# Two-layer HGRN2 + RWKV-7 trunk: the places of the conditioning columns, of the decay path's casts and of silu(c)

## The chip, the cores and the metric

The kernel runs on one NeuronCore of one Trainium2 chip. The metric is device time in microseconds (us) of one execution; the kernel is run several times and the median counts. Everything is float32; matmul operands are split into a high and a low part (`hi`, `lo`, both in the format fp32r), so that three matmuls (hi·hi, hi·lo, lo·hi) make one accurate product.

## What is computed

Two layers over 512 tokens of width 1024. Each layer first needs a conditioning vector of 3 × 1024 numbers from `c`:

```python
cond = silu(c) @ w_ada[l] + b_ada[l]
shift, scale, gate_raw = split(cond, 3)
h = x * (1 + scale) + shift
p_hg, p_rw, p_gate = split(h @ w_in[l], [...])
y_hg = HGRN2(p_hg) * silu(z_hg) @ w_branch_hg[l]
y_rw = RWKV7(p_rw) * silu(z_rw) @ w_branch_rw[l]
merged = sigmoid(g_hg) * y_hg + sigmoid(g_rw) * y_rw
x = layer_norm(ALPHA * x + (1 + gate_raw) * (merged @ w_out[l]))
```

`shift` and `scale` of a layer must be there before its projection starts. `gate_raw` is needed only at that layer's end. So in layer 0 the kernel has time to make layer 0's eight gate columns and layer 1's sixteen shift and scale columns (a column is 128 of the 1024 numbers, one per partition) beside other work.

## The kernel before, in words

**A column** (`ada_col`, line 308) is made on VectorE (DVE). A 128 × 1024 block of `w_ada` is loaded in two halves by two DMAs (`ada_next`, line 327, on the queue of SP). Each half is multiplied with half of silu(c) and summed along the row by one fused instruction (in the trace `CUSTOM_DVE_ANT_0`, in the order of instructions `ISA`), each followed by a short read of the accumulator, and a last small addition joins the halves. silu(c), copied to all partitions, lies in two tiles, `silc`. `ada_next` first computes the columns that are pending, then starts the loads of the next ones, so a column is loaded one call ahead of its use. Tiles named `z` (four of them) hold the halves.

**A layer** goes through these stages:

1. The four pairs. For `p` = 0 to 3 one HGRN2 head (`hg_head`) and one preparation of two RWKV heads (`rw_prep`) are made. Both are long chains of small steps on DVE, ScalarE (ACT), GpSimd (POOL) and TensorE (PE). Between the steps, `weave` places `fill`: matmuls of the projection tiles that come next (lines 267, 268 and 272), in numbers that tables set for each step. PE runs its instructions in that fixed order, so a late DVE step makes PE wait, and the fill behind it too. In the first pair `rw_wa` makes the RWKV decay and rate from the 64-wide down projections `wad`: two tiles `x[i]` get a cast of one half of the partitions (line 381) and a subtraction for the other half, and eight pairs of matmuls (lines 393, 394) read them.
2. `rw_invert`: a triangular inversion, all on DVE, with fill on PE.
3. Eight chunks (`rw_chunk`) of the RWKV recurrence, with fill; each makes one column in layer 0, its two halves pinned at two places (`side`).
4. The branch stage, for `j` = 0 to 7: two projections `pa` and `pb` (weights `w_br`), then on DVE two `SCALAR_TENSOR_TENSOR` that read them out of PSUM (lines 1170 and 1171, shown as line 135), their sum (line 1172) and `hilo`: ACT casts the high part, DVE subtracts for the low part (line 126). `out1(j - 1)` then multiplies the previous tile with the first half of `w_out`. Weights come through three `raw` tiles on SP's queue, are cast by ACT (line 121, `wh<-raw`), and POOL makes the low part (line 126, `wl<-raw,wh`).
5. The layer's end, which is joined with the start of the next layer.

**What sets the order.** The program is written as one stream per engine and a scheduler orders it by priority. `tc.issue_after(x)` makes the instructions of the block stand behind `x` if they are on the same engine as `x`. It adds no wait, and it does not bind other engines: the loads of a column may go earlier.

**The columns before.** In the pairs of layer 0 `ada_next` is called after each `weave` (lines 1075 and 1087), eight times for one column each (`WAZ`), and nothing pins those instructions. The scheduler put all eight of them in the stretch from the middle of the first pair to the beginning of the second. Eight more are made in the chunks, and eight in the branch stage (`WAB`), there behind the sum of line 1172 (`merged`).

**silu(c).** Before the chunks, ACT copies `silc` to two other tiles, `keep`, since the chunks use its memory. After the chunks `keep` is given up, and at the start of the branch stage `c` is loaded again (line 1161), spread over all partitions, and `c_rows` computes silu again: a tanh on ACT and a `SCALAR_TENSOR_TENSOR` on DVE for each half.

Of the kernel before, what the change touches and what calls it, by code (L numbers as in the profile page):

```python
# [12 lines left out]
F32 = mybir.dt.float32  # L13
F32R = mybir.dt.float32r
U8 = mybir.dt.uint8
AF = mybir.ActivationFunctionType
ALU = mybir.AluOpType
AX = mybir.AxisListType

WAZ = (1, 1, 1, 1, 1, 1, 1, 1)  # L20
WAB = (1, 1, 1, 1, 1, 1, 1, 1, 0)
NWARM = 5
ORD = ((11, 2), (3, 20), (4,), (5, 6), (21,7), (8,), (), ())

# [58 lines left out]
def body(ctx, tc, d):  # L83
# [20 lines left out]
    def u(shape=(128, 512), dt=F32):  # L104
        return st("u", list(shape), dt)

    def big(tag, dt=F32R):
        return st(tag, [128, 4, 2, 512], dt)
# [16 lines left out]
    def tt(e, o, a, b, op):  # L125
        return e.tensor_tensor(o, a, b, op=op)  # L126

    def mul(e, o, a, b):
        return tt(e, o, a, b, ALU.mult)
# [7 lines left out]
    def bc(ap, n):  # L137
        return ap.unsqueeze(len(ap.shape)).broadcast_to(list(ap.shape) + [n])
# [237 lines left out]
    def rw_wa(l, wad):  # L376

        x = [st("z", [128, 512], F32R) for _ in range(2)]
        for i in range(2):
            r, q = slice(64 * i, 64 * i + 64), slice(64 - 64 * i, 128 - 64 * i)  # L380
            V.tensor_copy(x[i][r], wad[r])
            tt(V, x[i][q], wad[r], x[i][r].bitcast(F32), ALU.subtract)
        wu = [wunit(d["up"][l, i], *(("X", "X") if l else ("pu", "pu"))) for i in range(2)]
        for i in range(2):

            G.memset(wu[i][1][64 - 64 * i:128 - 64 * i].bitcast(F32), 0.0)
        rw["gt"], rw["vm"] = [], []
        for p in range(NP):
            cols = slice(p * 128, (p + 1) * 128)
            g = st("t4" if p < 3 else "G", [128, 2, 512])  # L390
            for i, bias in ((0, "w0"), (1, "a0")):
                pw = ps("rw")
                yield mm(pw, wu[i][0][:, cols], x[i], start=True, stop=False)
                yield mm(pw, wu[i][1][:, cols], x[i], start=False, stop=True)
                act(g[:, i], pw, AF.Tanh, scale=0.5, bias=P(bias, l, p))
            rw["gt"].append(g)
# [22 lines left out]
        shift(x, pst, l, c)  # L419
        return x  # L420

    def rw_prep(l, p, r, k, v, after):

        sg, th = rw["gt"][p][:, 0], rw["gt"][p][:, 1]
        if l == 1:
# [8 lines left out]
        ts(G, sg, sg, 0.5, 0.5, ALU.mult, ALU.add)  # L434
        cum = pu()
        with tc.issue_after(after[0].ins):
            V.tensor_tensor_scan(cum, mask64, sg, 0.0, ALU.mult, ALU.add)
        EP = ep
        EI = cum
        with tc.issue_after(after[1].ins):  # L440
# [64 lines left out]
                mm(pA[h][ro:ro + 64, c4i * 64:(c4i + 1) * 64], ZR[hs, zc:zc + 64], BK[hs, zc:zc + 64],  # L505
                   start=c4i == 0, stop=c4i == 3)
        for h in range(2):
            mul(V, ar[:, h, p], pA[h][:, 0:256].rearrange("p (c j) -> p c j", j=64), bc(d2[:, :, p, h], 64))

        pT = ps("rw")  # L510
        for t in range(4):
# [174 lines left out]

    def hilo(y, o, e=G):
        act(o[:, 0], y, AF.Copy)
        tt(e, o[:, 1], y, o[:, 0].bitcast(F32), ALU.subtract)

    def rw_gate(l, p, pz):
        z, t = st("z", [128, 512]), u()
# [308 lines left out]
    for l in range(L):  # L1001
# [62 lines left out]
        for p in range(NP):  # L1064
            early = []
            if p:
                fill = itertools.chain(fqi(p, hgp), krv(p, rkv))
            elif l:
                fill = itertools.chain(fqi(p, hgp), wa(), krv(p, rkv))
            else:  # L1070
                fill = itertools.chain(krv(p, rkv), rw_wa(l, wad), fqi(1, early, 1))
            weave(hg_head(l, p, hgp, oT, ends := []), fill, (WHL if l else WHZ, WHG if l else WHS, WHG, WHG)[p])
            run(fill)
            if l == 0:
                ada_next(*itertools.islice(ada, WAZ[2 * p]))
            if p == 0:
                rw["vtm"] = [st("X", [128, 512]) for _ in range(8)]
            hgp = early
            if p < 3:
                fill = fqi(p + 1, hgp, 3 if early else 2)  # L1080
            else:
                fill = itertools.chain.from_iterable(
                    [gate(j) for j in range(5)] + [zrw(p) for p in range(NP)] + [zhg(p) for p in range(NP)] +
                    [gate(j) for j in range(5, KT)])
            weave(rw_prep(l, p, rkv[1], rkv[0], rkv[2], ends), fill, WPR)
            if l == 0:
                ada_next(*itertools.islice(ada, WAZ[2 * p + 1]))
            if p < 3:
                run(fill)
            rkv = []  # L1090
        ada_next()

        piece[:] = [512]
        keep = [hl(), st("pr", [128, 512])]
# [8 lines left out]
        for c in range(8):  # L1103
            ada_next(*itertools.islice(ada, 1), tag="u")
            weave(rw_chunk(l, c, ada_parts()), fill, WCH, 1000)
        o_hg, y_rw = big(tag_r), big(tag_r)

        def finish():
            with tc.high_priority(offset=1000):
# [46 lines left out]

        xa, ow, wo = [], [], []
        if l == 0:
            craw = [u(), u()]
            for h in range(2):  # L1160
                nc.sync.dma_start(craw[h], d["c"][h * 512:(h + 1) * 512].partition_broadcast(128))
            c_rows(craw)
            ada_next(*itertools.islice(ada, WAB[0]))
        if l == 1:
            n0, nrm = norm_rows(0), norm_rows(1)
        for j in range(KT):
# [4 lines left out]
            stt(mc, gates[j][1], 1.0, pb, ALU.add, ALU.mult)  # L1171
            merged = V.tensor_tensor(ma, ma, mc, op=ALU.add)
            with tc.issue_after(merged.ins):
                hilo(ma, mg[j], V)
            ow.append(wunit(d["w_out"][l, j * 128:(j + 1) * 128, 0:512]))
            if j:
                wo.append(wo_unit(j - 1))
                out1(j - 1)
            with tc.issue_after(merged.ins):
                if l == 0:  # L1180
                    ada_next(*itertools.islice(ada, WAB[j + 1]))
                elif j % 2 == 0:
                    x1_rows(j // 2)
# [210 lines left out]
```

## Time and profile before

| | |
|---|---|
| median of 3 runs | 996.07 us (994.84 to 997.43) |
| the profiled execution | 997.83 us, of which the span from the first to the last instruction is 996.0 us |
| mean granted clock of TensorE over the span | 0.977 of full speed |
| PE busy | 943.5 us (95% of the span) |
| DVE busy | 733.2 us (74%) |
| ACT, POOL busy | 453.8 us (46%), 602.9 us (61%) |

The pairs of layer 0 lie at about 57 to 230 us, its inversion to 283, its chunks to 390, its branch stage at 411 to 478; layer 1 starts at about 520. A row of a timeline gives start, duration, engine, line, operation, tiles and count, and in brackets how long the engine stood idle before it and which instruction ended that idle time. An idle time of PE costs time; an idle time of another engine costs time only where PE comes to wait for that engine. A matmul of 128 × 512 lasts 0.39 us in these rows at full clock, but the next starts before it ends.

### The profile page before, as it was taken

The numbers are of one execution on the slowest core, as the hardware profiler recorded it, in microseconds if no ns is written. First come the engines' busy times: TensorE is split into PE (matmuls) and PEld (weight loads), VectorE is DVE, ScalarE is ACT, GpSimd is POOL, SyncE is SP. The second block draws the span as 40 slices with busy tenths as digits, with TensorE's granted clock in tenths as the row PEclk, the third lists the DMA queues.
The fourth block names the chain that finished last, engine by engine and source line by source line (L and its number), as shares of the span: only waits on it lengthen the run. The fifth ranks groups of instructions, "written<-read, shape, count | busy, mean of one in ns | idle before, by whom it ended". The sixth has DMA issues, their size and how long they took to land.

```text
span 996.0 us, 16762 instructions
## 1 busy us (share of the span) xinstructions
PE 943.5 (95%) x6132; PEld 762.2 (77%) x6132; DVE 733.2 (74%) x1265; ACT 453.8 (46%) x924; POOL 602.9 (61%) x580
## 2 busy tenths in 40 slices
PE   7979899999998999999989999999999899999996
PEld 4757788887876777778878777888787677777775
DVE  7888986769974766487876686767899376746767
ACT  3356465465334335433444655555632443353421
POOL 5466657556445666666545577666642566675665
PEclk9998999999998999999999999999999899999998
DMA  9824332322322341656632122222231333355322
GB/s 315 315 64 148 116 86 75 92 74 85 99 76 84 98 117 44 173 187 190 193 119 64 54 85 85 75 82 77 75 96 64 96 107 97 108 171 166 114 78 84
DMA packets 61748, 112.83 MB, mean 113 GB/s; under 512 B 6865, under 2 KB 11361, under 8 KB 61666
## 3 DMA queue, kind: packets, MB, share of 16 engines
q1 hardware_dynamic: 57778, 105.12, 34.0%
q10 hardware_dynamic: 3888, 6.64, 2.0%
q8 instruction: 48, 0.79, 0.3%
q14 instruction: 34, 0.28, 0.1%
HBM read 106.49 MB, written 5.25 MB: 112 GB/s over the span
## 4 chain that ended last, share of the span: by engine, by line
PE 63%; DVE 25%; DMA 4%; ACT 3%; issue 3%; POOL 2%; SPq 0%; DVEq 0%; POOLq 0%; ACTq 0%
PE ppj L272 14%; PE ppj L267 13%; PE ppj L268 13%; DVE t L126 5%; DVE t L541 3%; DVE B L308 2%; DVE t L533 2%; PE prw L597 2%; DVE u L126 1%; POOL wl L126 1%; PE prw L616 1%; PE ppj L1194 1%; PE ppj L1196 1%; PE ppj L1195 1%; PE prw L621 1%
## 5 line engine op out<-in xcount | busy, mean ns | idle before, releaser
L126 POOL TENSOR_TENSOR wl<-raw,wh 128x256 fp32r<-128x256 f32 (+1 forms) x321 | 348.1, 1099 | 268.0 <-ACT wh L121 135.3
L121 ACT ACTIVATE wh<-raw 128x512 fp32r<-128x512 f32 (+1 forms) x233 | 144.1, 622 | 166.6 <-PE ppj L268 103.0
L267 PE MATMUL ppj<-B,wh 128*128 128x512 f32 x432 | 174.7, 404 | 1.8 <-DVE u L135 1.8
L268 PE MATMUL ppj<-B,wh 128*128 128x512 f32 x432 | 172.2, 399 | 0.0
L267 PE MATMUL ppj<-A,wh 128*128 128x512 f32 x400 | 163.1, 408 | 0.0
L268 PE MATMUL ppj<-A,wh 128*128 128x512 f32 x400 | 161.4, 403 | 0.0
L272 PE MATMUL ppj<-B,wl 128*128 128x512 f32 x432 | 125.5, 401 | 0.0
L272 PE MATMUL ppj<-A,wl 128*128 128x512 f32 x400 | 118.3, 407 | 2.4 <-POOL wl L126 2.4
L267 PEld LDWEIGHTS ppj<-B,wh 128*128 128x128 f32 x432 | 82.0, 190 | 18.9 <-ACT wh L121 2.6
L272 PEld LDWEIGHTS ppj<-B,wl 128*128 128x128 f32 x432 | 81.0, 190 | 17.1
L268 PEld LDWEIGHTS ppj<-B,wh 128*128 128x128 f32 x432 | 82.1, 190 | 14.9
L272 PEld LDWEIGHTS ppj<-A,wl 128*128 128x128 f32 x400 | 75.3, 193 | 20.2 <-POOL wl L126 4.5
L267 PEld LDWEIGHTS ppj<-A,wh 128*128 128x128 f32 x400 | 76.7, 192 | 16.0 <-ACT wh L121 0.3
L268 PEld LDWEIGHTS ppj<-A,wh 128*128 128x128 f32 x400 | 76.9, 192 | 14.1
L126 DVE TENSOR_TENSOR t<-t,t 128x144 f32<-128x144 f32 (+29 forms) x62 | 44.3, 715 | 2.1
L126 POOL TENSOR_TENSOR hl<-hl,u 128x256 f32<-128x256 f32 x40 | 32.0, 800 | 20.0 <-DVE u L787 9.2
L135 DVE SCALAR_TENSOR_TENSOR pr<-ppj,prm,pr 128x511 f32<-128x511 f32 x22 | 16.5, 748 | 30.2 <-ACT pr L123 30.2
L126 DVE TENSOR_TENSOR W<-prw,d 64x256 f32<-64x256 f32 x32 | 13.5, 422 | 33.7 <-PE prw L621 33.2
L126 DVE TENSOR_TENSOR hl<-hl,u 128x256 f32<-128x256 f32 x64 | 31.9, 519 | 2.6 <-ACT u L805 1.3
L516 ACT COPY X<-prw 64x128 f32<-64x128 f32 x64 | 16.7, 261 | 25.4 <-PE prw L512 24.7
L541 DVE TENSOR_REDUCE t<-t 128x4 f32<-128x4 f32 (+30 forms) x62 | 26.4, 425 | 2.1
L126 DVE TENSOR_TENSOR u<-u 128x256 f32<-128x256 f32 (+6 forms) x56 | 25.5, 456 | 0.7
(484 smaller groups left out, 2009.8 us busy)
## 6 DMA issues: line engine op xcount, KB each, us to landing
raw<-in_w_in SPq DMA_DIRECT2D x182, 256.0 KB, 2.6
B<-in_w_ada SPq DMA_DIRECT2D x16, 512.0 KB, 6.2
z<-in_w_ada SPq DMA_DIRECT2D x32, 256.0 KB, 3.4
u<-in_w_ada SPq DMA_DIRECT2D x32, 256.0 KB, 3.5
raw<-in_w_br SPq DMA_DIRECT2D x32, 256.0 KB, 2.7
raw<-in_w_out SPq DMA_DIRECT2D x32, 256.0 KB, 2.7
u<-in_x SPq DMA_DIRECT2D x8, 256.0 KB, 4.4
o<-in_w_in SPq DMA_DIRECT2D x14, 128.0 KB, 4.7
```

Source lines behind the costliest of these rows:

```text
L121: A.activation(out, in_, f, scale=scale)
L126: return e.tensor_tensor(o, a, b, op=op)
L135: V.scalar_tensor_tensor(o, a, s, b, op0=op0, op1=op1)
L267: yield mm(o, w, xh, start=half == 0 and k == 0, stop=False)
L268: yield mm(o, w, xl, start=False, stop=False)
L272: yield mm(o, w, xh, start=False, stop=half == n - 1 and k == 3)
L308: V.tensor_tensor_reduce(out=w[h], in0=w[h], in1=silc[h], scale=0.5, scalar=0.0 if h else init, op0=ALU.mult, op1=ALU.add, accum_out=part[ ...
L516: A.copy(rw["vtm"][2 * t + e][r:r + 64, p * 128:(p + 1) * 128], pT[64 * e:64 * e + 64, t * 128:(t + 1) * 128])
L533: V.transpose(Tin[qs].rearrange("p t s -> p s t"), ax[qs, :, cs_].rearrange("p h s -> p s h"))
L541: V.tensor_reduce(blk(R, t, [32, j]), pv, axis=AX.X, op=ALU.add)
L597: mm(pg[h][:, p * 128:(p + 1) * 128], BK[p][hs, ch], ZR[p][hs, ch], start=p == 0, stop=p == 3)
L616: mm(py[:, p * 128:(p + 1) * 128], ZR[p][:, ch], mbd[:, p], start=p == 0, stop=False)
```

## The change

There are four edits.

- **The columns in the pairs of layer 0.** `ada_next` is now called inside `rw_prep` at two places: `side(0)`, pinned behind the scan on DVE, and `side(1)`, pinned behind the last multiplication of the preparation (`ar`). `WAZ` starts five columns instead of eight, none at the first place of the first pair, and as a column is computed one call after its load, the first pair computes none. The other three are made later: the chunks still take eight, and `WAB` gives the branch stage eleven instead of eight, two at every second tile.
- **The branch stage's pins.** Columns (in layer 1, the rows of `x1`) stand behind the low part's subtraction (`low`) and no more behind `merged`.
- **The casts of the decay path** (line 381) go from DVE to ACT, in both layers.
- **silu(c)** is copied back from `keep` by ACT after the chunks, instead of being loaded and computed again.

```diff
-WAZ = (1, 1, 1, 1, 1, 1, 1, 1)
-WAB = (1, 1, 1, 1, 1, 1, 1, 1, 0)
+WAZ = (0, 1, 1, 1, 1, 1, 0, 0)
+WAB = (1, 2, 1, 2, 1, 2, 1, 1, 0)
...
             r, q = slice(64 * i, 64 * i + 64), slice(64 - 64 * i, 128 - 64 * i)
-            V.tensor_copy(x[i][r], wad[r])
+            act(x[i][r], wad[r], AF.Copy)
             tt(V, x[i][q], wad[r], x[i][r].bitcast(F32), ALU.subtract)
...
-    def rw_prep(l, p, r, k, v, after):
+    def rw_prep(l, p, r, k, v, after, side):
...
-            V.tensor_tensor_scan(cum, mask64, sg, 0.0, ALU.mult, ALU.add)
+            scan = V.tensor_tensor_scan(cum, mask64, sg, 0.0, ALU.mult, ALU.add)
+        with tc.issue_after(scan.ins):
+            side(0)
...
-            mul(V, ar[:, h, p], pA[h][:, 0:256].rearrange("p (c j) -> p c j", j=64), bc(d2[:, :, p, h], 64))
+            last = mul(V, ar[:, h, p], pA[h][:, 0:256].rearrange("p (c j) -> p c j", j=64), bc(d2[:, :, p, h], 64))
+        with tc.issue_after(last.ins):
+            side(1)
...
-        tt(e, o[:, 1], y, o[:, 0].bitcast(F32), ALU.subtract)
+        return tt(e, o[:, 1], y, o[:, 0].bitcast(F32), ALU.subtract)
...
-            if l == 0:
-                ada_next(*itertools.islice(ada, WAZ[2 * p]))
...
-            weave(rw_prep(l, p, rkv[1], rkv[0], rkv[2], ends), fill, WPR)
-            if l == 0:
-                ada_next(*itertools.islice(ada, WAZ[2 * p + 1]))
+            side = lambda i: ada_next(*itertools.islice(ada, 0 if l else WAZ[2 * p + i]))
+            weave(rw_prep(l, p, rkv[1], rkv[0], rkv[2], ends, side), fill, WPR)
...
-        ada_next()
...
         o_hg, y_rw = big(tag_r), big(tag_r)
+        if l == 0:
+            silc[:] = [mbd.rearrange("p a b -> p (a b)"), st("W", [128, 512])]
+            for h in range(2):
+                A.copy(silc[h], keep[h])
...
         if l == 0:
-            craw = [u(), u()]
-            for h in range(2):
-                nc.sync.dma_start(craw[h], d["c"][h * 512:(h + 1) * 512].partition_broadcast(128))
-            c_rows(craw)
             ada_next(*itertools.islice(ada, WAB[0]))
...
             with tc.issue_after(merged.ins):
-                hilo(ma, mg[j], V)
+                low = hilo(ma, mg[j], V)
...
-            with tc.issue_after(merged.ins):
+            with tc.issue_after(low.ins):
                 if l == 0:
                     ada_next(*itertools.islice(ada, WAB[j + 1]))
```

**DVE in the first pair of layer 0**, where the HGRN2 head begins (`hl`, `phg` and `prw` are its tiles, `z` the decay path's). Before:

```order
L126 TENSOR_TENSOR u_630<-u_605 128x256
L381 CAST z_706<-u_613 64x512
L126 TENSOR_TENSOR hl_628<-phg_669,cc 128x512
L787 COPY u_677<-hl_606 128x64x2
L126 TENSOR_TENSOR hl_627<-hl_627,u_630 128x128x2
```

and now:

```order
L126 TENSOR_TENSOR u_630<-u_605 128x256
L126 TENSOR_TENSOR z_706<-u_613,z_706 64x512
L126 TENSOR_TENSOR hl_628<-phg_669,cc 128x512
L792 COPY u_677<-hl_606 128x64x2
L126 TENSOR_TENSOR hl_627<-hl_627,u_630 128x128x2
```

The cast has left DVE, and the decay path's subtraction stands in its place. PE's two `L792` matmuls of that level, which need the copy, now stand behind three matmuls of line 272 instead of one.

**SP's queue in the branch stage of layer 0**, where the tiles' weights (`raw`) and the columns (`z`) are loaded. Before:

```order
L1150 DMA raw_4426<-in_w_out 128x512
L327 DMA z_4448<-in_w_ada 128x512
L327 DMA z_4449<-in_w_ada 128x512
L252 DMA raw_4453<-in_w_br 128x512
L252 DMA raw_4472<-in_w_br 128x512
L252 DMA raw_4497<-in_w_out 128x512
```

and now:

```order
L1155 DMA raw_4404<-in_w_out 128x512
L327 DMA z_4349<-in_w_ada 128x512
L327 DMA z_4350<-in_w_ada 128x512
L327 DMA z_4426<-in_w_ada 128x512
L327 DMA z_4427<-in_w_ada 128x512
L252 DMA raw_4435<-in_w_br 128x512
L252 DMA raw_4454<-in_w_br 128x512
L252 DMA raw_4479<-in_w_out 128x512
```

Four halves of columns now stand ahead of the next tile's two `w_br` loads where two stood. This comes three times in the stage; between them it is two as before.

**DVE at the start of layer 1's branch stage** (`B` is the tile of `hilo`, `bv` and `o` are the rows of `x1`, `raw` is the second half of `w_out`, which this layer multiplies with the gate row `X`). Before:

```order
L1172 TENSOR_TENSOR u_9168<-u_9168,u_9169 128x512
L126 TENSOR_TENSOR bv_9181<-bv_9181,z_9114 128x512
L126 TENSOR_TENSOR o_9185<-o_9185,z_9115 128x512
L126 TENSOR_TENSOR bv_9181<-bv_9181,z_9116 128x512
L126 TENSOR_TENSOR o_9185<-o_9185,z_9117 128x512
L126 TENSOR_TENSOR B_9112<-u_9168,B_9112 128x512
L135 SCALAR_TENSOR_TENSOR u_9227<-hl_7352,ppj_9189 128x512
L126 TENSOR_TENSOR raw_9240<-raw_9240,X_9105 128x512
```

and now:

```order
L1173 TENSOR_TENSOR u_9162<-u_9162,u_9163 128x512
L126 TENSOR_TENSOR raw_9234<-raw_9234,X_9099 128x512
L135 SCALAR_TENSOR_TENSOR u_9221<-hl_7346,ppj_9183 128x512
L126 TENSOR_TENSOR B_9106<-u_9162,B_9106 128x512
L126 TENSOR_TENSOR bv_9175<-bv_9175,z_9108 128x512
L126 TENSOR_TENSOR o_9179<-o_9179,z_9109 128x512
```

The rows of `x1` now follow the low part, as the new pin asks, but the multiplication of `raw` has come ahead of it.

## Rows read from the trace of the kernel before

**Rows 1.** The page's chain that ended last: shares of the span by engine

```profile
PE 63%; DVE 25%; DMA 4%; ACT 3%; issue 3%; POOL 2%; SPq 0%; DVEq 0%; POOLq 0%; ACTq 0%
```

**Rows 2.** Windows, first pairs of both layers: busy us (instructions), PEclk, DMA share, GB/s

```profile
60.00:120.00 60.00, 50.03 (x259) 39.83 (x258) 54.80 (x110) 32.42 (x76) 39.40 (x47) 0.92 0.44 136
530.00:590.00 60.00, 56.21 (x317) 45.71 (x317) 46.79 (x77) 35.60 (x79) 39.05 (x46) 1.00 0.23 67
```

**Rows 3.** Timeline of DVE in the first pair of layer 0

```profile
70.05 2.60 DVE L381 CAST z<-u 64x512 fp32r<-64x512 f32 x1
72.57 0.67 DVE L126 TENSOR_TENSOR hl<-phg,cc 128x512 f32<-128x512 f32 x1
73.17 0.21 DVE L787 COPY u<-hl 128x128 f32<-128x128 f32 x1
...
75.76 0.69 DVE L126 TENSOR_TENSOR z<-u,z 64x512 fp32r<-64x512 f32 x1
```

**Rows 4.** Timeline of POOL at the same place

```profile
70.27 2.09 POOL L126 TENSOR_TENSOR wl<-raw,wh 128x256 fp32r<-128x256 f32 x3
```

**Rows 5.** Waits of PE, 55 to 130 us: us in total, times, longest

```profile
PE prw L792 <- DVE u L787: 3.2, 1, 3.2
PE phg L763 <- DVE u L126: 2.6, 3, 1.6
PE prw L505 <- DVE B L135: 1.6, 1, 1.6
PE prw L816 <- ACT u L808: 1.0, 1, 1.0
```

**Rows 6.** Timeline of PE: matmuls before and after a wait

```profile
113.23 0.39 PE L267 MATMUL ppj<-A,wh 128*128 128x512 f32 x1
113.46 0.39 PE L268 MATMUL ppj<-A,wh 128*128 128x512 f32 x1
...
117.44 0.63 PE L267 MATMUL ppj<-A,wh 128*128 128x512 f32 x1
117.87 0.63 PE L268 MATMUL ppj<-A,wh 128*128 128x512 f32 x1
```

**Rows 7.** Windows of line 308 alone on DVE, 60 to 122 us: sum

```profile
sum 62.00, DVE 13.66; mean DVE 4.55
```

**Rows 8.** Timeline of DVE in the third pair and at the fourth's start

```profile
171.69 0.69 DVE L126 TENSOR_TENSOR pu<-pr,pu 128x512 f32<-128x512 f32 x1 [1.32 <-POOL pu L132]
...
193.10 0.50 DVE L126 TENSOR_TENSOR u<-u,u 128x256 f32<-128x256 f32 x1 [2.71 <-ACT u L730]
```

**Rows 9.** Timelines of DVE and PE, start of layer 0's branch stage

```profile
417.85 0.69 DVE L135 SCALAR_TENSOR_TENSOR mbd<-mbd,u 128x512 f32<-128x512 f32 x1 [2.92 <-ACT mbd L123]
...
421.38 0.47 PE L267 MATMUL ppj<-B,wh 128*128 128x512 f32 x1 [1.82 <-DVE u L135]
...
426.42 0.50 PE L1131 MATMUL prw<-wh,A 128*128 128x512 f32 x1 [1.58 <-DVE A L126]
```

**Rows 10.** Timelines of DVE and PE, decay path of layer 1

```profile
543.14 1.75 DVE L381 CAST z<-u 64x512 fp32r<-64x512 f32 x2
...
545.67 0.50 PE L393 MATMUL prw<-z,X 128*128 128x512 f32 x1 [2.02 <-DVE z L126]
```

**Rows 11.** Layer 0's branch stage: a cast on ACT, its first matmul, landings of `raw`

```profile
435.25 0.63 ACT L121 ACTIVATE wh<-raw 128x512 fp32r<-128x512 f32 x1 [3.27 <-DMA raw<-in_w_br]
...
437.02 0.39 PE L267 MATMUL ppj<-B,wh 128*128 128x512 f32 x1
...
DMA to landing us min/median/max: 2.3/2.7/4.6
```

**Rows 12.** Timelines of DVE and PE, start of layer 1's branch stage

```profile
907.05 0.68 DVE L126 TENSOR_TENSOR B<-u,B 128x512 fp32r<-128x512 f32 x1
...
908.25 0.68 DVE L126 TENSOR_TENSOR raw<-raw,X 128x512 f32<-128x512 f32 x1
...
907.78 0.50 PE L1131 MATMUL prw<-wh,B 128*128 128x512 f32 x1 [0.26 <-DVE B L126]
```

## The prediction

> **What bounds the kernel now.** I read the chain that ended last first: PE holds 63% of the span and DVE 25% [rows 1]. So the kernel is PE's fixed list of matmuls, with stretches in which PE waits for a DVE chain. A microsecond taken off DVE is worth something only where PE stands idle behind it. The second view is the windows, for two stretches of equal length and nearly equal work: the first pair of layer 0, where columns run, and the first pair of layer 1, where none do [rows 2]. In the first PE is idle for 60.00 − 50.03 = 10.0 us and gets 0.92 of its clock; in the second it is idle for 3.8 us at 1.00. The reader is to see in that pair of rows what the columns and their neighbours cost at most: 6.2 us of idle time and 0.08 × 60 = 4.8 us of clock, 11.0 us in all. The third view, PE's waits, names the culprit: the long ones of this stretch end on DVE [rows 5].
>
> All sums are made against the profiled execution, 997.83 us, which is 1.8 us above the median of the three runs.
>
> **The casts of layer 0, first pair.** PE's longest wait, 3.2 us, is for the copy of line 787 [rows 5]. On DVE that copy stands behind a cast that took 2.60 us [rows 3], while POOL was busy with three splits from 70.27 to 72.36 [rows 4]. The cast goes to ACT. In its place stands the subtraction (0.69), then 0.67 and 0.21 [rows 3]: from 70.05 that ends at 71.6 instead of 73.38. **−1.8 us**. Bounds: 0, if the subtraction takes as long as the cast did, and −2.6, the whole cast. I take the subtraction at its own row. The Trainium skill, page SBUF — State Buffer, section Who interferes with whom, says that DVE and GpSimd share one port pair, that it is an exclusive lock, and that a DVE operation with two SBUF inputs contends with a GpSimd one that reads SBUF; by that rule the subtraction waits as the cast did and this term is near 0, which is the first rival below.
>
> **The slow clock behind that wait.** After PE's waits of 3.2 and 1.6 us matmuls start 0.43 us apart (117.44 to 117.87) instead of 0.23 (113.23 to 113.46) [rows 6], the lower of the two clock levels (1.2 instead of 2.4 GHz), for some 12 and 11 matmuls: 12 × 0.2 = 2.4 us and 2.2 us. That agrees with the 4.8 us of clock above. If the waits shrink, I expect both stretches gone: **−4.6 us**. Bounds: 0 to −4.8. The wait at line 505 was as long (1.6) and lies in the same stretch, and no slow matmuls follow it, so a wait of some 1.4 us that is left need not cost clock.
>
> **The columns in the first pair.** Line 308 takes 13.66 us of DVE in these 62 us [rows 7], all in or beside the chain for which PE waits. They leave the first pair altogether. The waits for DVE steps among which they stand are 2.6 + 1.6 us, and 1.0 us on ACT that was itself fed late by DVE [rows 5], 5.2 in all. Some of line 763's (its first one, before any column) stays: **−4.6 us**. Bounds: −2.3 (half) to −5.2. Together with the casts and the clock this makes −11.0, the same as the comparison with layer 1.
>
> **The columns in the later pairs.** Five columns (13.66 / 8 = 1.7 us each) come back, pinned. Behind the scan DVE next waits 1.32 us for POOL anyway, and behind `ar` it stands idle for 2.71 us at the next head's start [rows 8]. The second place covers a column; at the first the rest, 0.4 us, goes into later idle time of the chain. **0**. If all that cover were gone: 5 × 1.7 = +8.5. The loads are a whole place ahead of their use.
>
> **silu(c).** At the start of layer 0's branch stage DVE waits 2.92 us for ACT's tanh, which waits for `c`; the reading of `pb` out of PSUM stands behind, so PE waits 1.82 us for its bank and then 1.58 us for the low part [rows 9]. Load, tanh and DVE step all go. The two `A.copy` run while the last chunk's fill is on PE. **−3.4 us**. Bounds: −1.8 (the second wait stays) to −3.4; if the copies' cover is gone they cost 2 × 0.63, by the cast's row [rows 11].
>
> **The casts of layer 1.** PE waits 2.02 us at line 393, behind two casts of 1.75 us together [rows 10]. ACT needs some time for the two as well, so I take a good half: **−1.2 us**. Bounds: 0 to −1.8.
>
> **The branch stage's queue in layer 0.** Three more columns are made here, and three times four halves stand ahead of two `w_br` loads instead of two. Weights come just in time: a cast ends at 435.88, its first matmul starts at 437.02 [rows 11], a margin of 1.1 us. A landing takes 2.7 us in the middle and 4.6 at most [rows 11], so two more halves ahead cost up to 1.9, less the margin 0.8, three times 2.4. **+1.5 us**, nearer to the upper end as other margins may be smaller. Bounds: 0 and +5.7 (no margin). The extra columns themselves fit DVE's idle time; the low part now goes first.
>
> **Layer 1's branch stage.** The low part ended at 907.73 and PE's matmul waited 0.26 us for it [rows 12]. It now stands behind the multiplication of `raw`, which needs the gate row and started at 908.25 [rows 12]; the low part may end near 909.5, up to 1.8 us later. Part of that PE would lose later to weights. **+0.8 us**. Bounds: −0.5 to +1.8.
>
> Sum: −1.8 − 4.6 − 4.6 − 3.4 − 1.2 + 1.5 + 0.8 = −13.3, so 984.5 us against the profiled execution and 982.8 against the median. I predict **983 us**.
>
> **The rivals.**
>
> *The next late thing takes over in the first pair* (chance 0.20). The subtraction is held where the cast was, or POOL's splits hold the matmuls of line 272 that now stand ahead of line 792. Then the 1.8 us and the slow stretch behind (2.4) stay, and half of the column term (2.3): −13.3 + 6.5 = −6.8, so 989 to 991. For it: POOL was busy until 72.36 [rows 4]. Against it: layer 1's first pair has such casts too and is idle for 3.8 us only [rows 2].
>
> *SP's queue starves the branch stage: slower than before* (chance 0.05). SP's queue is one list, and a load that waits for a free `z` tile holds the weights behind it; that tile is freed by DVE's columns, which now stand later. Price: the four weight loads of a double tile each come 1.9 us late [rows 11], 7.6 less the margin of 1.1, so 6.5 each, three times 19.5. Instead of the +1.5 of the sum: 997.83 − 14.8 + 19.5, about 1002. It decides from the point where a `w_br` takes over 2.7 + 1.1 = 3.8 us from issue to landing on every double tile. Against it: the stage's loads show 4.6 once as the maximum [rows 11]. The Trainium skill, page DMA: Bandwidth & Descriptors, section Queues, rings and completion order, says that each DMA engine consumes a queue's descriptors in ring order; by that rule the weights do wait for all four halves, and no row shows four ahead.
>
> *The pinned columns lie on the path after all: no change* (chance 0.07). Then the five cost 8.5 us instead of 0, and with part of the first rival the gain is 0 to 3 us, 994 to 997. Against it: the idle times beside both places [rows 8].
>
> *More than I count* (chance 0.08). Both branch terms come to nothing and the column term is whole: −16.2 or a little more, 979 to 976.
>
> That the change does something other than it says is ruled out by the order of the instructions: no column stands in the first pair, and no load of `c` in the branch stage.
>
> **How the numbers follow.** My forecast, 979 to 989, has 0.60. A measurement of this kernel can tell from no change what differs by over 0.3%, 3.0 us, so faster means under 993.1. That holds for the forecast, the first rival and the larger gain: 0.60 + 0.20 + 0.08 = 0.88. Same is the third rival, 0.07. Slower is the second, 0.05. The range, 976 to 992, leaves out the second rival, most of the third and a little of the tails, some 0.15.
>
> **What would show it.** Right: PE's idle time in 60 to 120 us falls from 10.0 to about 4, the clock there is 1.00, and the second pair begins some 10 us earlier; the wait at line 792 is under 1.5 us; the wait for `c` is gone; the branch stage shows new waits of 2 us at most. Wrong: the wait at line 792 stays near 3 us with a subtraction of over 2 us before it (first rival); PE waits for `wh` or `wl` on every second branch tile (second); PE waits at line 505 or 763 in the later pairs (third).

## The result, and the profile after

The changed kernel takes **1001.33 us** (median of 6 runs, 1000.46 to 1005.07), the kernel before 995.43 us in the same comparison (6 runs, 991.86 to 997.43): a ratio of **1.0068**, 95% interval 1.0044 to 1.0092. It is slower by some 6 us where 13 us less was forecast. The profiled execution has a span of 1001.1 us, 5.1 more than that of before, and the two traces can be laid beside each other. The table gives the start of the first matmul of each place on PE (from line 505 on, lines of the changed kernel are 1 to 5 higher than before), and what had been gained or lost by then.

| place | before | after | after less before |
|---|---|---|---|
| first head, layer 0 | 67.52 | 67.49 | 0.0 |
| second head | 115.64 | 108.81 | −6.8 |
| line 505 (now 508) of the second pair | 145.43 | 137.82 | −7.6 |
| inversion | 281.79 | 274.17 | −7.6 |
| last chunk | 380.14 | 371.35 | −8.8 |
| second `out1` | 434.30 | 422.32 | −12.0 |
| `out2` | 478.08 | 482.40 | **+4.3** |
| line 505 of layer 1's first pair | 579.20 | 581.92 | +2.7 |
| first `out1`, layer 1 | 906.91 | 908.61 | +1.7 |
| end | 996.04 | 1001.12 | +5.1 |

So the first pair gave 7.6 us and silu(c) about 3.2; then layer 0's branch stage took 16.3 us back in 60, and layer 1's another 3.4.

**Gained.** The windows of the first pairs, as in [rows 2]:

```profile
60.00:120.00 60.00, 55.35 (x305) 46.04 (x304) 48.97 (x90) 38.43 (x93) 41.12 (x52) 0.94 0.29 88
530.00:590.00 60.00, 57.29 (x337) 47.81 (x336) 43.08 (x70) 37.40 (x80) 40.12 (x47) 1.00 0.25 71
```

PE's idle time in the first fell from 10.0 to 4.65 us, but the clock rose only from 0.92 to 0.94. The long wait did not go. PE's waits (55 to 130 us), then DVE's and POOL's timelines at that place, answer to [rows 5], [rows 3] and [rows 4]:

```profile
PE prw L797 <- DVE u L792: 3.4, 1, 3.4
```

```profile
69.67 0.69 DVE L126 TENSOR_TENSOR hl<-phg,cc 128x512 f32<-128x512 f32 x1
70.27 3.24 DVE L792 COPY u<-hl 128x128 f32<-128x128 f32 x1
```

```profile
70.20 0.72 POOL L126 TENSOR_TENSOR wl<-raw,wh 128x256 fp32r<-128x256 f32 x1
70.86 0.52 POOL L386 MEMSET pu<- 64x512 f32 x1
71.35 2.08 POOL L126 TENSOR_TENSOR wl<-raw,wh 128x256 fp32r<-128x256 f32 x3
```

The cast is gone from DVE, and the copy that used to last 0.21 us lasts 3.24 in its stead, until POOL's run ends at 73.43.

**Lost.** PE's waits between 410 and 485 us, and SP's for the loads of columns:

```profile
PE ppj L267 <- ACT wh L121: 12.2, 4, 5.5
```

```profile
SPq L327 <- DVE sm L308: 18.3, 14, 4.2
```

In the same stretch of the kernel before, PE had no wait for `wh`, and SP's same wait (for `z`, on line 308) came to 3.5 us. One tile shows how it goes. DVE's timeline from the sum of line 1173 on, then SP's, ACT's and PE's:

```profile
417.34 0.69 DVE L1173 TENSOR_TENSOR u<-u,u 128x512 f32<-128x512 f32 x1
418.73 0.69 DVE L126 TENSOR_TENSOR A<-u,A 128x512 fp32r<-128x512 f32 x1 [0.70 <-ACT A L121]
419.34 1.80 DVE L308 CUSTOM_DVE_ANT_0 z<-z,mbd,prm 128x512 f32<-128x512 f32 x1
...
424.54 0.68 DVE L308 CUSTOM_DVE_ANT_0 z<-z,W 128x512 f32<-128x512 f32 x1
```

```profile
421.17 4.40 SPq L327 DMA_DIRECT2D z<-in_w_ada  x4
425.68 1.14 SPq L252 DMA_DIRECT2D raw<-in_w_br  x2
```

```profile
430.00 0.63 ACT L121 ACTIVATE wh<-raw 128x512 fp32r<-128x512 f32 x1 [9.13 <-DMA raw<-in_w_br]
```

```profile
430.69 0.80 PE L267 MATMUL ppj<-B,wh 128*128 128x512 f32 x1 [5.48 <-ACT wh L121]
431.28 0.63 PE L268 MATMUL ppj<-B,wh 128*128 128x512 f32 x1
431.70 0.63 PE L267 MATMUL ppj<-B,wh 128*128 128x512 f32 x1
```

Both columns of the double tile stand behind the low part (418.73). Each half that ends frees one `z` tile, and SP's next load goes out at that moment: the first at 421.17 (a half ended at 421.14, as DVE's row has it), the fourth at 425.25. The two `w_br` behind them in SP's list go out at 425.68 and 426.49 and land after 4.2 and 4.5 us. ACT has waited 9.13 us for the first, PE waits 5.48. Behind the wait the matmuls start 0.43 us apart, the lower clock level, until 434.68, some nine of them. In the DMA view of 413 to 485 us, a `w_br` takes 4.3 us from issue to landing in the middle, before 2.6. PE's four waits make 12.2 of the 16.3 us; the slow clock (0.83 from 420 to 440, 0.91 from 460 to 480) goes with the rest.

Layer 1's loss is at the start of its branch stage, as in [rows 12]; DVE and PE:

```profile
909.47 0.69 DVE L126 TENSOR_TENSOR raw<-raw,X 128x512 f32<-128x512 f32 x1 [4.16 <-DMA X<-in_lnb]
...
910.67 0.69 DVE L126 TENSOR_TENSOR B<-u,B 128x512 fp32r<-128x512 f32 x1
```

```profile
911.41 0.50 PE L1136 MATMUL prw<-wh,B 128*128 128x512 f32 x1 [2.19 <-DVE B L126]
```

The low part now stands behind the multiplication of `raw`, for which DVE waited 4.16 us. It ends at 911.36, 1.9 us later than before when the stage's start (1.7 us later) is taken off. PE waits 2.19 us instead of 0.26, and its clock is 0.86 from 908 to 920 (before, from 906 to 918, 1.00).

### The profile page after: what moved, and what is told of

Its sections match the earlier page's. It is cut to its first block, busy times and chain, and to the rows that moved or that the text cites. A ratio compares the mean times of both kernels' runs of the same rounds, so it can differ in the third digit from the quotient of the medians.

```text
span 1001.1 us, 16760 instructions
## 1 busy us (share of the span) xinstructions
PE 943.6 (94%) x6132; PEld 763.2 (76%) x6132; DVE 739.6 (74%) x1259; ACT 456.3 (46%) x928; POOL 606.3 (61%) x580
## 4 chain that ended last, share of the span: by engine, by line
PE 57%; DVE 24%; DMA 4%; issue 4%; ACT 2%; POOL 2%; SPq 0%; ACTq 0%; DVEq 0%; POOLq 0%
PE ppj L272 13%; PE ppj L267 13%; PE ppj L268 12%; DVE t L126 4%; DVE t L546 3%; DVE z L308 3%; DVE t L538 2%; POOL wl L126 2%; DMA raw<-in_w_br 2%; PE prw L602 2%; PE prw L621 1%; PE prw L797 1%; DVE u L126 1%; PE prw L639 1%; DVE u L135 1%
## 5 line engine op out<-in xcount | busy, mean ns | idle before, releaser
L267 PE MATMUL ppj<-B,wh 128*128 128x512 f32 x432 | 176.8, 409 | 12.7 <-ACT wh L121 12.2
L268 PE MATMUL ppj<-B,wh 128*128 128x512 f32 x432 | 173.9, 403 | 0.0
L126 DVE TENSOR_TENSOR hl<-hl,u 128x256 f32<-128x256 f32 x64 | 35.8, 578 | 3.5 <-ACT u L789 2.0
L126 DVE TENSOR_TENSOR A<-u,A 128x512 fp32r<-128x512 f32 x16 | 15.7, 979 | 23.7 <-ACT A L121 23.7
```

What stands on the lines that cost most here:

```text
L267: yield mm(o, w, xh, start=half == 0 and k == 0, stop=False)
L268: yield mm(o, w, xl, start=False, stop=False)
```

## The experiments

"The stage" is the time from the second `out1` to `out2` in layer 0: before 43.8 us, after 60.1. Ratios are to the kernel before, with 95% intervals. A stage or a place is read from one trace of each kernel, and traces differ: before and e12, whose instructions are the same up to the last chunk, lie 0.9 us apart at the second pair (eight kernels with the change's first pair only 0.3), and six kernels with e1's order of the branch stage (e1, e5, e6, e11, e13, e14) show 43.5 to 46.0 us for it. Less than about 1 us at a place in the pairs, or 2.5 in the stage, is not shown by one trace.

### The branch stage: pins, columns, tiles

**e1, the merged pin** (the changed kernel with one edit undone):

```diff
-            with tc.issue_after(low.ins):
+            with tc.issue_after(merged.ins):
                 if l == 0:
                     ada_next(*itertools.islice(ada, WAB[j + 1]))
```

> The changed kernel with one edit undone: in the branch stages the columns (layer 0) and the rows of x1 (layer 1) are pinned behind the merged sum again, not behind its low part; the double columns stay. The changed kernel takes 69.1 us from the first out1 to out2 in layer 0 (before: 53.9), and its layer 1 stage is 3.1 us longer than before. Closed chain (weights wait in SP's list behind a column's load, this for a z tile, this for the column, this for the low part, this for ACT's cast, which stands behind the cast of a late weight): the columns no longer stand behind ACT, so about 8 of the 15.2 us come back, and the 3.1 of layer 1: 989 to 992 us against 1001. Bytes (four halves ahead of the weights are too much for the queue): the layer 0 stage stays at 68 to 69 us, only layer 1 comes back: 997 to 998. DVE's time (two columns in a tile are too much for DVE): the low part now comes behind two columns, the stage stays or gets longer: 998 to 1001.

Measured: 985.03 us, ratio 0.9888 (0.9861 to 0.9915). The stage takes 44.9 us and layer 1's from the first `out1` to the end 89.6 (before 89.1, after 92.5). More came back than any theory had said. So the double columns are harmless behind `merged`: neither their bytes nor their time on DVE make the loss by themselves. The same tile in this version, DVE's timeline and SP's:

```profile
416.11 1.16 DVE L1173 TENSOR_TENSOR u<-u,u 128x512 f32<-128x512 f32 x1
417.19 0.74 DVE L308 CUSTOM_DVE_ANT_0 z<-z,mbd,prm 128x512 f32<-128x512 f32 x1
...
418.47 0.68 DVE L126 TENSOR_TENSOR A<-u,A 128x512 fp32r<-128x512 f32 x1
...
420.24 1.86 DVE L308 CUSTOM_DVE_ANT_0 z<-z,mbd,prm 128x512 f32<-128x512 f32 x1
```

```profile
417.96 0.94 SPq L327 DMA_DIRECT2D z<-in_w_ada  x2
420.33 0.33 SPq L252 DMA_DIRECT2D raw<-in_w_br  x1
422.14 2.02 SPq L327 DMA_DIRECT2D z<-in_w_ada  x2
424.60 0.33 SPq L252 DMA_DIRECT2D raw<-in_w_br  x1
```

Two things differ. The first column runs in the gap in which DVE otherwise waits for ACT's cast, so the first tile comes free 0.7 us after the sum and not 3.1. And the scheduler wrote another list for SP: `z z`, `w_br`, `z z`, `w_br` in place of `z z z z`, `w_br`, `w_br`.

**e2 and e3, single columns**, with the pin behind `low` and behind `merged`:

```diff
-WAZ = (0, 1, 1, 1, 1, 1, 0, 0)
-WAB = (1, 2, 1, 2, 1, 2, 1, 1, 0)
+WAZ = (0, 1, 2, 1, 2, 1, 1, 0)
+WAB = (1, 1, 1, 1, 1, 1, 1, 1, 0)
```

> The changed kernel with one column in each tile of layer 0's branch stage, as before, and the three others in pairs 1 and 2 (two columns behind the preparation there). The pin behind the low part stays. Closed chain through the z tiles, bytes, DVE's time: all three say that the stage from out1 to out2 comes back from 69.1 to 54 to 56 us; the price of three more columns in the pairs is 0 by their cover and at most 3 x 1.7 = 5: 986 to 992. If the pin behind the low part alone costs (a theory in which the doubling is innocent), the stage stays over 64 us and the time over 996.

> Both edits of the two kernels beside it: single columns in the branch stage, three more in the pairs, and the pin behind the merged sum in both layers. If the two causes add, it is faster than the single columns alone by the 3.1 us of layer 1: 983 to 989. If the pin matters only beside double columns, the layer 0 stage is as in the single columns and only layer 1 differs.

Measured: 993.42 us, ratio 0.9982 (0.9967 to 0.9996), stage 48.7; and 985.45 us, ratio 0.9900 (0.9877 to 0.9922), stage 44.4. The pin costs 4.3 us with single columns and 15.2 with doubles; doubles cost 11.4 behind `low` and nothing that can be told (0.5) behind `merged`. e2 is a little slower than forecast (986 to 992). Eight columns in the pairs instead of five lost 2 to 3 us by the inversion, of which 1.3 to 2.3 are left by the second chunk; yet e3 and e1 take the same time (985.45 and 985.03), so which place is better for the three is not shown.

**e4, tiles of its own** for the second column of a double:

```diff
-            w = [st(tag, [128, 512]) for _ in range(2)]
+            w = [st(tag if i == 0 else second, [128, 512]) for _ in range(2)]
...
-                    ada_next(*itertools.islice(ada, WAB[j + 1]))
+                    ada_next(*itertools.islice(ada, WAB[j + 1]), second="o")
```

> The changed kernel with double columns and the pin behind the low part, but the second column of a double tile is loaded into tiles of its own (those of the o buffers, free in this stage), so that no load of a column waits for a column of the same tile. Bytes, loads and DVE's work are the same. Closed chain through the z tiles: 11 to 13 of the stage's 15.2 lost us come back, 988 to 990. Bytes: the stage stays at 68 to 69 us, 1000 to 1001. DVE's time: no change either, 1000 to 1001. Between (stage about 60): each has a share.

Measured: 992.39 us, ratio 0.9969 (0.9952 to 0.9987), stage 49.2: 10.9 of the 15.2 us come back with every DVE instruction in its place, so DVE's time is not what hurts behind `low` either. But the loads did not stay in theirs. SP's timeline, in the last chunk and at the first double tile:

```profile
374.53 4.53 SPq L327 DMA_DIRECT2D o<-in_w_ada  x4
...
420.40 2.03 SPq L327 DMA_DIRECT2D z<-in_w_ada  x2
422.52 0.86 SPq L252 DMA_DIRECT2D raw<-in_w_br  x2
423.47 0.38 SPq L252 DMA_DIRECT2D raw<-in_w_out  x1
423.94 0.86 SPq L327 DMA_DIRECT2D o<-in_w_ada  x2
```

With free tiles the scheduler moved four of the six extra halves to 374 us and the other two to 424, and no `w_br` stands behind four halves any more. So the doubles hurt through their loads, but e4 does not tell the late tile from the place in SP's list; e9 and e10 do.

**e8, the high part on DVE**, to cut the way over ACT's queue:

```diff
-                low = hilo(ma, mg[j], V)
+                V.tensor_copy(mg[j][:, 0], ma)
+                low = tt(V, mg[j][:, 1], ma, mg[j][:, 0].bitcast(F32), ALU.subtract)
```

> The changed kernel with double columns in the four z tiles and the pin behind the low part, but the high part of the merged tile is cast on DVE instead of ACT, so that the low part and the columns behind it no longer stand behind ACT's queue. DVE gets 0.7 us more in each tile. Closed chain over ACT (its cast of the merged tile stands behind the cast of a weight that is late): the chain is cut, the stage from the second out1 to out2 in layer 0 falls from 60.1 to 45 to 49 us: 986 to 990 us in all. Chain closed without ACT (it is enough that the columns stand behind low and share tiles): the stage stays above 56, over 997.

Measured: 997.70 us, ratio 1.0016 (0.9999 to 1.0034), stage 60.3. My link over ACT fell: nothing of the stage comes back. (From layer 1's first `out1` to the end it takes 89.9 us here instead of 92.5, so there the cast on ACT did matter: with the cast on DVE the low part, from 905.42, stands ahead of `raw`, from 910.73.)

**e9 and e10, SP's list and DVE's order apart.** e9 has the pin behind `low`, DVE's order of the changed kernel and e1's list, but for one `w_out` load that stands ahead of a column's two halves at the first tile; e10 has e1's order on every other engine and the list of the changed kernel, but for the same exchange:

```diff
+            if l == 0 and j > 1:
+                with tc.issue_after(loads[-1].ins):
+                    ada_load(itertools.islice(ada, WAB[j]))
             pb = run(proj([d["w_br"][l, j, 1]]
```

```diff
+            ahead = l == 0 and j in (3, 5, 7)
+            if ahead:
+                ada_load(itertools.islice(ada, 1))
+            with tc.issue_after(loads[-1].ins) if ahead else contextlib.nullcontext():
                 pa = run(proj([d["w_br"][l, j, 0]]
```

> The changed kernel (columns behind the low part, doubles, four z tiles) with one thing moved: on SP the load of a double tile's first column stands behind the first w_br load of the next tile, so that the list reads z z, w_br, z z, w_br where the changed kernel has z z z z, w_br, w_br. That is the list which the merged-pin version has by itself. DVE's order is that of the changed kernel. If the pin did its harm through SP's list (a weight stands behind the load that waits for the last z tile), the stage from the second out1 to out2 falls from 60.1 to 45 to 50 us and the time to 987 to 991. If the harm is that the columns run later (z tiles come free later whatever the list), it stays above 56, over 997.

> The reverse: the merged-pin version (985.0 us; columns ahead of the low part), with DVE's, ACT's, POOL's and PE's orders untouched, and SP's list as in the changed kernel: in the next tile but one after each double the first w_br stands behind the load for the last z tile. Through SP's list: the stage from the second out1 to out2 rises from 44.9 to 53 to 60 us, 993 to 1000. Through the columns' place on DVE: it stays at 45 to 47, 985 to 987. If both are needed: it rises by a few us, 988 to 991.

Measured: 990.98 us, ratio 0.9959 (0.9940 to 0.9979), stage 49.5; and 992.13 us, ratio 0.9968 (0.9946 to 0.9991), stage 51.8. PE's waits for `wh` in e9, then in e10 (its lines are one to five higher):

```profile
PE ppj L267 <- ACT wh L121: 4.1, 4, 1.7
```

```profile
PE ppj L268 <- ACT wh L122: 5.7, 3, 2.7
```

| | SP: `w_br` between | SP: `w_br` last |
|---|---|---|
| DVE: columns from `merged` on | 44.9 (e1; SP waits 9.6 for `z`) | 51.8 (e10; 11.6) |
| DVE: columns behind `low` | 49.5 (e9; 14.7) | 60.1 (the change; 18.3) |

The list alone costs 6.9 us (between the forecasts for e10), the place on DVE alone 4.6, both together 15.2. That is a weight held in SP's list behind a load that waits for a tile: how long the tile is late (DVE), and whether the weight stands behind it (SP). The first double tile shows it in the time from the sum to the issue of the first `w_br`: 3.1 us in e1, 5.3 in e9, 7.0 in e10, 7.7 in the change. That the two work on each other (15.2 is 3.6 more than their sum) rests on four single traces and is not far above what traces differ by.

### The first pair

**e6 and e7, casts and columns apart.** e6 is e1 with the casts back on DVE. e7 is the kernel before with casts on ACT and silu(c) copied back, its columns and pins untouched.

```diff
-            act(x[i][r], wad[r], AF.Copy)
+            V.tensor_copy(x[i][r], wad[r])
```

> The changed kernel with the pin behind the merged sum (985.0 us), and the casts of the low-rank input back on DVE, in both layers. By the terms of the prediction this gives back 1.8 us of waiting and 2.4 us of slow clock in layer 0 and 1.2 in layer 1: 990. Held by POOL's run: in layer 0 the wait ends with POOL's run whichever DVE instruction stands in it, so nothing is given back there, and in layer 1 the 1.5 us that the changed kernel gains between the third head mark and line 505: 986 to 987.

> The kernel before with two parts of the change alone: the casts on ACT and silu(c) copied back. Columns, pins and the branch stages are as before. By the terms of the prediction: 1.8 + 2.4 (clock behind the wait) + 1.2 + 3.4 = 8.8 us faster than before, ratio 0.991. Held by POOL's run: 0 + 1.5 + 3.4 = 4.9 us, ratio 0.995. What the merged-pin version gains beyond this (ratio 0.9888, so 11.2 us) is then the columns' leaving the first pair.

Measured: 987.46 us, ratio 0.9907 (0.9883 to 0.9931), and 986.95 us, ratio 0.9900 (0.9877 to 0.9924). e7's median fits my forecast of 8.8 us, but its trace does not show it in that place: there only 0.9 us is gained by the second pair, and 7.7 over the span. e12 below, with the casts left on DVE, shows the same 0.9, so the casts give nothing there. e6 has gained 6.9 us there without the casts, and e1 (with both) 7.5, at the third pair 6.9. So in layer 0 the columns' leaving is worth 6.0 to 6.9 us (against e12 and before), the slow clock of 100 to 120 us with it (0.93 before, 1.00 in e6), and the casts 0 to 0.7. In layer 1 the stretch from the first head to line 505 takes 40.5 us in e1 and e7, with the casts on ACT, and 42.1, 43.1 and 43.1 in before, e6 and e12, with the casts on DVE: there they are worth 1.6 to 2.6. By the medians e7 is 4.4 us faster than e12; its profiled execution was the slowest of its six (990.16), and where the rest of that lies is not shown.

**e5, e13, e11, e14: what holds the copy.** All stand on e1. e5 puts that one copy on ACT; e13 the two zero fills of line 386; e11 puts the splits of the up weights on DVE; e14 is e11 with e13's edit.

```diff
-                PK[e](kp.rearrange(
+                (A.copy if l + p + n == 0 else PK[e])(kp.rearrange(
```

```diff
-            G.memset(wu[i][1][64 - 64 * i:128 - 64 * i].bitcast(F32), 0.0)
+            q = slice(64 - 64 * i, 128 - 64 * i)
+            if l:
+                G.memset(wu[i][1][q].bitcast(F32), 0.0)
+            else:
+                act(wu[i][1][q], wu[i][0][q].bitcast(F32), AF.Copy, scale=0.0)
```

```diff
-        wu = [wunit(d["up"][l, i], *(("X", "X") if l else ("pu", "pu"))) for i in range(2)]
+        wu = [wunit(d["up"][l, i], *(("X", "X") if l else ("pu", "pu")), G if l else V) for i in range(2)]
```

> The changed kernel with the pin behind the merged sum (985.0 us) and one more edit: in the very first head, at its first level, the second of line 792's two copies goes to ACT instead of DVE. In the changed kernel that copy takes 3.24 us on DVE, from 70.27 to 73.5, and ends with a run of POOL's splits (until 73.43); PE waits 3.4 us for it and is slow behind it for some 2.4 us. Held by POOL's run: on ACT the copy takes 0.3 us, and PE's wait at 73.66 goes; but the next level's keys come from a multiplication in POOL's queue behind the same splits (73.66 to 74.5), so PE waits again some 2 us later: a gain of 1 to 2 us, 983 to 984, or up to 5 if the clock stays up as well, 980. Not held, but late for its data: the copy is as late on ACT, no gain, 985.

> The merged-pin version with the two splits of the low-rank up weights of layer 0 (the pu tiles, 2.1 us on POOL from 68.1 on) on DVE, 0.7 us each. If POOL's run of splits, from 68.1 to 73.4, holds DVE's copy of line 792, the run is now 2 us shorter or ends sooner and the copy and PE's wait of 3.4 us end 1.5 to 2 us sooner: 983 us, and less slow clock. If the splits, now on DVE ahead of the copy, are themselves held by POOL's other three, nothing is gained: 985, or it is 1 us slower.

> The merged-pin version (985.0 us) with one thing moved: the two zero fills of layer 0's low-rank up weights (line 386) go from POOL to ACT. POOL keeps all its splits. In the profiles with a long wait, the DVE instruction that is held (2.59, 3.25 and 3.16 us) starts beside or just behind POOL's zero fill and ends with the run of splits that follows; in the version with the splits of the up weights on DVE the fill stands elsewhere, and DVE and POOL take turns, one instruction each. The fill lets POOL's run go on without a turn: here they take turns, the copy of line 792 ends near 71 instead of 73.5, PE's wait of 3.4 us falls under 1.5, 983 us or less. The run of splits alone holds DVE (its length decides): the copy ends near 73, the wait stays near 3, 985.

> The fastest version so far (splits of the up weights of layer 0 on DVE, merged pin, 980.8 us) with the zero fills on ACT too. PE waits 1.0 us for a zero fill there, and 1.7 us for DVE's part of the same input: if the fill is the later of the two, up to 1 us is gained, 980; if DVE's part ends last in any case, nothing, 981.

Measured: e5 984.80 us, ratio 0.9883 (0.9862 to 0.9904), no gain over e1: a later DVE instruction, the next but one, is held instead, and PE waits 4.6 us at line 393. DVE's timeline of e5:

```profile
70.25 0.93 DVE L126 TENSOR_TENSOR hl<-hl,u 128x256 f32<-128x256 f32 x1
71.10 3.16 DVE L126 TENSOR_TENSOR u<-u 128x128 f32<-128x128 f32 x1
```

e13, with all splits still on POOL and DVE's order as in e1 (on POOL one multiplication, `hl`, now stands ahead of the last two splits): DVE, then POOL:

```profile
70.27 0.73 DVE L796 COPY u<-hl 128x128 f32<-128x128 f32 x1
70.92 0.96 DVE L126 TENSOR_TENSOR hl<-hl,u 128x256 f32<-128x256 f32 x1
```

```profile
70.19 1.41 POOL L126 TENSOR_TENSOR wl<-raw,wh 128x256 fp32r<-128x256 f32 x2
71.57 0.93 POOL L126 TENSOR_TENSOR hl<-hl,u 128x256 f32<-128x256 f32 x1
```

The copy starts at the same time and lasts 0.73 us instead of 3.24; it is over at 71.00, before the exchanged multiplication begins. PE's wait there falls from 3.4 to 0.9, and the clock from 60 to 80 us is 1.00 (before and after 0.83, e1 0.91). e13 took 983.26 us, ratio 0.9891 (0.9874 to 0.9909): not to be told from e1 by its ratio, as new waits of 2.4 and 1.4 us came behind; its trace gains 0.8 us in this pair. e11 took **980.84 us**, ratio 0.9855 (0.9838 to 0.9872), in its trace 2.1 us ahead of e1 by the second head; it beats both kernels. e14 took 982.00 us, ratio 0.9879 (0.9861 to 0.9897): PE's wait for the fill is gone, and nothing is gained over e11.

### silu(c) alone

**e12** is the kernel before with these two pieces only:

```diff
+        if l == 0:
+            silc[:] = [mbd.rearrange("p a b -> p (a b)"), st("W", [128, 512])]
+            for h in range(2):
+                A.copy(silc[h], keep[h])
...
-            c_rows(craw)
```

> The kernel before with silu(c) copied back instead of reloaded, and nothing else of the change. By the prediction's term: 3.4 us faster than before (ratio 0.9966), in the stretch from the last chunk to the second out1 of layer 0. By its lower bound (the second wait stays): 1.8 us.

Measured: 991.34 us against 995.27, ratio 0.9967 (0.9951 to 0.9982), with a trace that gains 4.0 us from the last chunk to the second `out1`.

## Why the prediction was wrong, step by step

- **The branch stage's queue, +1.5 us: the step that failed, by 15 us** (16.3 in the trace, 12.2 of it PE's waits for `wh`). It took the loads as issued when due and priced what four halves ahead of the weights cost in landing. Landing did get longer (4.3 us in the middle, over the 3.8 that I named), but the larger part lies before the issue: SP stood before loads that had no tile (18.3 us instead of 3.5), and the first `w_br` of a double tile was issued 7.7 us after the sum, in e1 3.1. The two sentences on which it rested, that the extra columns fit DVE's idle time and that the low part now goes first, concern DVE alone. Neither asked when the columns free their tiles, and what SP holds back until then. The bound of +5.7 had the same gap. The prediction has no row of SP's waits for `z`. The rule that I cited from the Trainium skill, page DMA: Bandwidth & Descriptors, section Queues, rings and completion order, is about descriptors that are in a ring already; the trace's hold comes before that, in SP's list of instructions.
- **The second rival named this mechanism**, down to the held list, the columns that stand later and PE's waits for `wh`. It got 0.05 because the only row set against it was one of landings, which says nothing of a load that is not yet issued. That it came so close in time (1002, measured 1001) is in part luck: its price, 19.5 us, was also made of landings, 3.2 more than the stage lost, and the other terms gave less than I had counted. Nor did its price see that the pin decides it: it counted the double tiles, and e1 shows doubles harmless, e2 the pin costly without them.
- **Layer 1's branch stage, +0.8 (at most 1.8):** the place and the cause were right, the size was 3.4 by the trace (wait 2.19 us instead of 0.26, and slow clock behind it). The low part came as late as my upper bound had it (909.5, and 1.7 for the later start); what I left out was the clock.
- **Casts of layer 0 and the slow clock behind, −1.8 and −2.4:** failed; 0 to 0.7 by the traces. I took the cast's 2.60 us to leave with the cast; it was a hold, and another instruction beside POOL's run inherited it. The first rival came true in part: not the subtraction was held (1.11 us) but the copy behind it. By the rule of the Trainium skill that I had cited, page SBUF — State Buffer, section Who interferes with whom, one side blocks for the whole instruction of the other; the trace agrees that DVE is blocked, but shows one DVE instruction blocked over five of POOL's.
- **Columns leaving the first pair, −4.6, and the second slow stretch, −2.2:** right, 6.0 to 6.9 by e6.
- **Pinned columns in later pairs, 0:** right; the gain stays at 7.6 from the second pair to the inversion. **silu(c), −3.4:** right, 3.3 by e12's ratio. **Casts of layer 1, −1.2:** right, 1.6 to 2.6.
- Without the pin behind `low` (e1) the time is 985 us, inside the range that was given. Its trace is 12.8 us shorter than before, where the terms without the two of the branch stages add up to 15.6; the casts of layer 0 alone are 3.5 us or more short of their 4.2.

## What to carry to other kernels

When an edit moves the *reader* of a buffer, look for the load that waits for that buffer, and for what stands behind that load in its queue: price the late release by the queue's waits, not by the landing of what was issued. A pin that is free for its own engine may also make a scheduler rewrite another engine's list, so compare every list that feeds the stage. Where one engine's short instruction lasts ten times its usual time, find what the other engines run at that moment (here POOL) before counting that time as work that can be moved.

## What the runs showed of the hardware

- A DVE instruction stood 2.60 us before the change ([rows 3]), 3.24 after it and 3.16 in e5, each time from beside or up to 0.6 us ahead of POOL's zero fill (0.52 us) until the run of splits behind the fill was over; in e5 0.8 us longer, over POOL's next instruction too. With the fill on ACT (e13), or at another time (e11), DVE and POOL took turns, and in the 3 us from the copy on no DVE instruction lasted over 1 us. A run of splits alone does not hold DVE: in e11 POOL ran four of them while DVE's instructions beside them lasted 0.69 to 0.96 us. Where e11's second fill went, one DVE instruction is held again, until POOL's next two are over. e11's POOL at the copy, then POOL and DVE at the fill:

```profile
68.92 3.41 POOL L126 TENSOR_TENSOR wl<-raw,wh 128x256 fp32r<-128x256 f32 x4 [1.45 <-PE phg L768]
...
77.69 0.60 POOL L386 MEMSET pu<- 64x512 f32 x1
78.26 0.64 POOL L126 TENSOR_TENSOR hl<-hl,u 128x256 f32<-128x256 f32 x1
78.87 0.61 POOL L132 TENSOR_SCALAR t<-t 128x512 f32<-128x512 f32 x1
...
78.09 1.44 DVE L126 TENSOR_TENSOR u<-u 128x32 f32<-128x32 f32 x1
```

  Not every fill does it: beside that of line 534 and the splits behind it (99.63 to 102.45 in the changed kernel) DVE's two-input operations last 0.4 to 0.7 us. Why a fill should cost DVE its turn is not shown; only that moving this one ended the hold.
- The same half of a column takes 0.74 us (417.19, e1) or 1.8 (419.34, the change). The traces say what the long ones wait for: in all 16 traces each half that lasts 1.2 us or more (42 of 96 in the changed kernel) ends 0.53 to 0.57 us after an instruction of POOL ends. Above, three halves end at 421.14, 422.83 and 424.54, and POOL's three splits at 420.59, 422.28 and 423.99:

```profile
419.29 1.30 POOL L126 TENSOR_TENSOR wl<-raw,wh 128x512 fp32r<-128x512 f32 x1 [3.81 <-ACT wh L121]
420.54 1.74 POOL L126 TENSOR_TENSOR hl<-raw,hl 128x512 fp32r<-128x512 f32 x1
422.25 1.74 POOL L126 TENSOR_TENSOR wl<-raw,wh 128x512 fp32r<-128x512 f32 x1
```

  So POOL's splits are a part of why the `z` tiles came free late in the change: three of its four halves ran beside them, e1's first two in a gap of POOL's. No run moved those splits to try it.
